# Loading the first group of a rotation in eight transfers of every eighth row

## The chip, the cores and the metric

One core of one Trainium2 chip. The metric is the device time of one execution in microseconds (us), median of several runs. The span in a profile is the time from the first to the last instruction, some 1.8 us shorter than the device time here.

## The reference

```python
x: float32 [32, 3, 256, 256]
return np.rot90(x, k=2, axes=(-2, -1))      # each 256 x 256 image turned by 180 degrees
```

An image of 65,536 elements is simply reversed. 25.17 MB are read and 25.17 MB written, and there is no arithmetic. x and the result lie in HBM, the chip's main memory. The tiles of the kernel lie in SBUF, the core's on-chip memory, and have 128 partitions each. DMA engines move the data between the two; the page counts 16 of them.

## The kernel before

The 96 images are three groups of 32. An image is cut into four rows of 16,384 elements (64 KB), so a group is a tile of 128 partitions, one row each. VectorE reverses each row inside its partition (three copies for each of four pairs of pieces), and the store puts the four rows of an image back in reverse order. Three tiles A, Bt and Ct hold the three groups.

```python
def load(t, g, lo, hi, queue=nc.sync):
    return queue.dma_start(out=t[:, lo:hi], in_=x4[g][:, lo:hi])
...
TAIL = 1536
HEAD = 512
load(A, 0, 0, HEAD, nc.scalar)          # ACT's queue: 512 columns of every row
load(A, 0, HEAD, E)                     # SyncE's queue: the rest
load(Bt, 1, 0, E)
body = load(Ct, 2, 0, E - TAIL)
load(Ct, 2, E - TAIL, E)
inside(A)                               # VectorE, twelve copies
store(A, 0, 0, LEAD)
first = store(A, 0, LEAD, E)            # made to wait for body
...                                     # then inside and store for Bt and Ct
```

## Time and profile before

| | before |
|---|---|
| device time | 122.06 us (121.93 to 122.1, 3 runs) |
| span | 120.2 us |
| busy share of the DMA engines | 97.6% |
| busy share of VectorE | 37% |
| a row of 64 KB on one DMA engine | 2.42 us |

Read it as a stream: six group transfers (three loads, three stores) of about 19.35 us, one behind the other, with about 1.75 us ahead of the first data and 1.4 us behind the last. VectorE's work lies beside it. The profile's lines are shown in the prediction.

### The profile page before, as it was taken

What the parts mean: (1) busy time and instruction counts of PE and PEld (TensorE: products, weight loads), DVE (VectorE), ACT (ScalarE), POOL (GpSimd) and SP (SyncE); (2) the same over time, 40 slices, a digit from 0 to 9 for tenths busy, and PEclk for the clock granted to TensorE, in tenths of its full rate; (3) what the DMA queues carried; (4) which work ended last, traced back from release to release, by engine and by line L of the source; (5) the groups of instructions that cost most, each with busy time, mean ns of one, the idle gap of its engine ahead of it and who ended that gap; (6) DMA issues with size and microseconds to landing.
All of it is one profiled execution on the core that took longest, in us unless ns stands there. A gap on an engine that the chain in (4) does not pass through costs nothing.

```text
span 120.2 us, 97 instructions
## 1 busy us (share of the span) xinstructions
DVE 44.2 (37%) x36; POOL 0.2 (0%) x4
## 2 busy tenths in 40 slices
DVE  0000000499995099999059999500000000000000
POOL 0000000000000000000000000000000000000000
DMA  9888988899889879979499777988898889888990
GB/s 338 349 349 349 698 349 349 360 654 393 349 349 633 382 316 553 395 316 633 178 452 693 346 346 346 693 349 349 349 698 349 349 349 698 349 349 349 654 393 0
DMA packets 1296, 50.33 MB, mean 419 GB/s; under 512 B 144, under 2 KB 272, under 8 KB 528
## 3 DMA queue, kind: packets, MB, share of 16 engines
q1 hardware_dynamic: 1152, 50.07, 97.0%
q10 hardware_dynamic: 144, 0.26, 0.6%
HBM read 25.17 MB, written 25.17 MB: 419 GB/s over the span
## 4 chain that ended last, share of the span: by engine, by line
DMA 34%; DVE 25%; another core or an unknown queue 4%; issue 1%; SPq 0%; DVEq 0%
DMA Bt<-in_x_dram 34%; DVE T L52 8%; DVE Bt L52 8%; DVE Ct L52 8%; SPq L55 0%; DVEq L52 0%
## 5 line engine op out<-in xcount | busy, mean ns | idle before, releaser
L52 DVE COPY T<-A 128x2048 f32<-128x2048 f32 x4 | 4.9, 1226 | 22.7 <-DMA A<-in_x_dram 22.6
L52 DVE COPY T<-Ct 128x2048 f32<-128x2048 f32 x4 | 4.9, 1227 | 4.5 <-DMA Ct<-in_x_dram 4.4
L52 DVE COPY T<-Bt 128x2048 f32<-128x2048 f32 x4 | 4.9, 1226 | 4.4 <-DMA Bt<-in_x_dram 4.3
L52 DVE COPY Bt<-Bt 128x2048 f32<-128x2048 f32 x4 | 4.9, 1227 | 0.1
L52 DVE COPY A<-A 128x2048 f32<-128x2048 f32 x4 | 4.9, 1227 | 0.1
L52 DVE COPY A<-T 128x2048 f32<-128x2048 f32 x4 | 4.9, 1227 | 0.1
L52 DVE COPY Bt<-T 128x2048 f32<-128x2048 f32 x4 | 4.9, 1227 | 0.1
L52 DVE COPY Ct<-T 128x2048 f32<-128x2048 f32 x4 | 4.9, 1227 | 0.1
L52 DVE COPY Ct<-Ct 128x2048 f32<-128x2048 f32 x4 | 4.9, 1227 | 0.1
L100 POOL MEMSET const-bfloat16-1.0<- 128x1 bf16 x1 | 0.1, 101 | 0.0
L100 POOL MEMSET const-uint8-127<- 128x1 uint8 x1 | 0.1, 101 | 0.0
L100 POOL MEMSET const-float32-0.0<- 128x1 f32 x1 | 0.1, 98 | 0.2 <-issue 0.2
L100 POOL MEMSET const-float32-1.0<- 128x1 f32 x1 | 0.1, 98 | 0.0
## 6 DMA issues: line engine op xcount, KB each, us to landing
out_dram<-A SPq DMA_DIRECT2D x1, 8128.0 KB, 21.1
A<-in_x_dram SPq DMA_DIRECT2D x1, 7936.0 KB, 21.9
Ct<-in_x_dram SPq DMA_DIRECT2D x1, 7424.0 KB, 57.9
Ct<-in_x_dram SPq DMA_DIRECT2D x1, 768.0 KB, 59.3
A<-in_x_dram ACTq DMA_DIRECT2D x1, 256.0 KB, 22.0
out_dram<-A SPq DMA_DIRECT2D x1, 64.0 KB, 35.2
Bt<-in_x_dram SPq DMA_DIRECT2D x1, 40.8
out_dram<-Bt SPq DMA_DIRECT2D x1, 39.8
```

The source lines that it names most:

```text
L52: tc.keep_in_program_order(nc.vector.tensor_copy(out=dst, in_=src))
L100: nc = _bacc.Bacc("TRN2", target_bir_lowering=False, num_devices=1)
```

## The change

Its intent, as far as the code tells it: a first transfer of 16 rows has one row for each of the 16 DMA engines, so they might be fed sooner than by a transfer of 128 rows; and ACT's small strip becomes needless. Strip b holds the rows b, b + 8, ..., b + 120, on both sides.

```diff
     def load(t, g, lo, hi, queue=nc.sync):
-        return queue.dma_start(out=t[:, lo:hi], in_=x4[g][:, lo:hi])
+        return tc.keep_in_program_order(
+            queue.dma_start(out=t[:, lo:hi], in_=x4[g][:, lo:hi]))
...
     TAIL = 1536
-    HEAD = 512
-    load(A, 0, 0, HEAD, nc.scalar)
-    load(A, 0, HEAD, E)
+    for b in range(8):
+        tc.keep_in_program_order(
+            nc.sync.dma_start(out=A[b::8, :], in_=x4[0][b::8, :]))
     load(Bt, 1, 0, E)
```

## The prediction

That a row takes 4.84 us, twice 2.42, is an estimate of mine; nothing in the trace of the kernel before shows two engines slowing each other. Nor does it show the 132 us of the second rival.

> **What bounds the kernel now.** I read the page first: span, busy shares, DMA row, queues.
>
> ```profile
> span 120.2 us, 97 instructions
> DVE 44.2 (37%) x36; POOL 0.2 (0%) x4
> ...
> q1 hardware_dynamic: 1152, 50.07, 97.0%
> q10 hardware_dynamic: 144, 0.26, 0.6%
> HBM read 25.17 MB, written 25.17 MB: 419 GB/s over the span
> ```
>
> VectorE works for 44 of 120 us, the DMA engines for 97.0 + 0.6 = 97.6%. q1 is SyncE's queue, q10 ACT's, and q10 carries only the head strip (0.26 MB). The bytes cannot shrink: everything is read once and written once. So the kernel is a stream, and a change shows only where it adds a gap or changes the rate. The windows view, cut at the boundaries of the transfers, shows both (columns: stretch, length, VectorE and POOL busy, clock, DMA share, GB/s; a packet counts where it starts).
>
> ```profile
> 0.00:1.70 1.70, 0.00 (x0) 0.20 (x4) 1.00 0.00 0
> 1.70:21.78 20.08, 0.00 (x0) 0.00 (x0) 1.00 1.00 417
> 21.78:41.15 19.37, 14.72 (x12) 0.00 (x0) 1.00 1.02 440
> ...
> 80.11:99.45 19.34, 0.00 (x0) 0.00 (x0) 1.00 1.00 434
> 99.45:118.80 19.35, 0.00 (x0) 0.00 (x0) 1.00 1.00 434
> 118.80:120.20 1.40, 0.00 (x0) 0.00 (x0) 1.00 0.01 0
> ```
>
> Line two is the first group (8.39 MB), line three the second, the next two are stores. A full-rate group takes 19.35 us, 434 GB/s, which is 27.1 GB/s for each of 16 engines. A group is 128 rows of 64 KB, eight per engine, so a row takes 19.35 / 8 = 2.42 us. The first group takes 0.7 us more (20.08). Finer windows say where:
>
> ```profile
> 0.00:1.75 1.75, 0.00 (x0) 0.20 (x4) 1.00 0.00 0
> 1.75:2.75 1.00, 0.00 (x0) 0.00 (x0) 1.00 2.89 952
> 2.75:3.75 1.00, 0.00 (x0) 0.00 (x0) 1.00 0.15 63
> 3.75:4.75 1.00, 0.00 (x0) 0.00 (x0) 1.00 0.00 0
> 4.75:7.17 2.42, 0.00 (x0) 0.00 (x0) 1.00 1.00 433
> ```
>
> Nothing moves before 1.75; the first row of each engine occupies it to about 4.75, 3.0 us in place of 2.42; then it is steady. So the avoidable time in this kernel is about 1.75 us of start, 0.6 us of first row and 1.4 us of end, 3.7 us together. Last, who waits for the data (the timeline):
>
> ```profile
> 0.73 0.39 SPq L55 DMA_DIRECT2D A<-in_x_dram  x1
> 1.18 0.42 SPq L55 DMA_DIRECT2D Bt<-in_x_dram  x1
> ...
> 22.62 1.23 DVE L52 COPY T<-A 128x2048 f32<-128x2048 f32 x1 [22.62 <-DMA A<-in_x_dram]
> ```
>
> One issue costs SyncE about 0.45 us (0.73 to 1.18). VectorE starts when all of the first group has landed and finishes its twelve copies at about 37.7, well before the store of that group can flow at 60: queue order puts all loads ahead of the stores. VectorE is not on the path.
>
> [...]
>
> **The change, part by part.**
>
> Removed: ACT's strip of 512 columns. Its bytes now ride in the full rows. 0.26 MB at 434 GB/s is 0.6 us, against 0.6% of 120.2 = 0.7 us for q10: a saving of at most 0.1 us.
>
> Moved: the first issue is smaller (16 rows, not 128). If the engines are fed sooner by it, the start shrinks by some tenths; the issue is 0.39 us long, so I take 0.1 to 0.3 us, a guess.
>
> Added: seven more transfers. 8 issues x 0.45 = 3.6 us on SyncE, all during the first rows: an issue comes every 0.45 us, an engine uses one up in 2.42 us. The compiled order also shows new waits: [...] the second group's load now waits for the first strip, the third group's two parts for the second and third strip, the first store for the others. When the first strip lands, seven are still queued, at least 7 x 2.42 = 17 us of work: no gap. VectorE's first copy waits for eight landings in place of two, the last of which is the end of the group as before. Seven more completions per engine: I allow 0.1 us.
>
> Changed without being named: which partitions are written together. Strip b covers partitions b, 8+b, ..., 120+b. For b = 0 these are 0, 8, 16, 24, then 32, 40, 48, 56, then 64 and so on. [...] a row takes 4.84 us, the group 8 x 4.84 = 38.7 us, plus the 0.6 us of the first row, against 20.08 - 0.08 now: +19.3 us.
>
> Nothing hides this. The loads are one queue, so everything behind starts 19.3 us later: first copy near 41.9, second group landed near 60, third near 80, stores from 80 to 138. VectorE again finishes each group before its store's turn, so nothing else is added and nothing is recovered. Sum: 122.06 + 19.3 + 0.1 - 0.2 = 141.3 us.
>
> **The rivals.**
>
> *[...] 121.9 us.* If what limits at 27.1 GB/s is the DMA engine alone [...] the stage takes 19.4 + 0.6, and only the edges move, a few tenths. [...] I give this 0.19.
>
> *A conflict that sorts itself out: about 132 us.* [...] this, or a partial conflict, makes the low end of my range.
>
> *A starved queue.* If the new semaphore waits or eight short transfers left gaps, each strip would add up to the 0.8 us between the end of the first group's packets and the copy (21.78 to 22.62), 6 us in all. Against it: strips are queued before earlier ones land. Chance small.
>
> *Fewer engines than 16 per strip*: time would be in the hundreds; I give it one per cent, within "slower".
>
> *Faster by 2%* needs 2.4 us out of 3.7 us of edges, most of which (first data at 1.75, completion at the end) the change does not touch: 0.01.
>
> **Range and chances.** Slower has all the conflict cases: 0.80. Most of it is the fair case, 139 to 143; the unfair or partial ones spread to 130. [...] I set the top at 144. Range 130 to 144, which leaves out the case of no conflict knowingly.
>
> **What would show it.** Right: the first group's load at about 217 GB/s with DMA share still near 1 (packets twice as long, not gaps), VectorE's first copy near 41.9 us, second group and stores at 434 GB/s and 19.35 us as before; span near 139.5. Wrong: the first copy at about 22.5 (no conflict), or at about 32 (sorted out). [...] If the DMA share falls under 0.9 in the first stage, it is the queue that starves. If the first packets come well before 1.75, the smaller first issue is worth more than I took.

## The result, and the profile after

143.47 us (143.29 to 143.64, 6 runs) against 122.01 us for the kernel before in the same rounds: 21.5 us slower. The ratio is 1.176 (95% interval 1.174 to 1.178). A ratio here is the mean time of one kernel's fast runs over that of the other's of the same rounds, so not quite the ratio of the medians quoted. Predicted were 141.3 us.

The page of the changed kernel, the same lines as before:

```profile
span 141.6 us, 108 instructions
DVE 44.2 (31%) x36; POOL 0.2 (0%) x4
...
q1 hardware_dynamic: 1264, 50.33, 97.6%
HBM read 25.17 MB, written 25.17 MB: 355 GB/s over the span
```

The DMA engines are as busy as before, 97.6% of a span that is 21.4 us longer, for the same bytes. So no gap was added: the packets themselves take longer. The windows view says which (stretch, length, VectorE, POOL, clock, DMA share, GB/s):

```profile
0.00:2.10 2.10, 0.00 (x0) 0.20 (x4) 1.00 0.00 0
...
6.40:11.51 5.11, 0.00 (x0) 0.00 (x0) 1.00 1.00 205
11.51:16.62 5.11, 0.00 (x0) 0.00 (x0) 1.00 1.00 205
16.62:21.73 5.11, 0.00 (x0) 0.00 (x0) 1.00 1.00 205
21.73:26.64 4.91, 0.00 (x0) 0.00 (x0) 1.00 1.01 214
26.64:31.75 5.11, 0.00 (x0) 0.00 (x0) 1.00 1.00 205
...
41.97:61.32 19.35, 14.72 (x12) 0.00 (x0) 1.00 1.03 434
```

Each line of the middle is one strip: the 16 engines take one row each, in 5.11 us in place of 2.42, at 205 GB/s in place of 434. The fifth strip takes 4.91 us; that is a clue for later. The last line is the second group, at full rate again. And the first line shows that no data moves before 2.10 us: the start became later than the 1.75 us of before, not earlier.

The timeline at the start and at VectorE's first copy:

```profile
0.73 5.05 SPq L72 DMA_DIRECT2D A<-in_x_dram  x8
8.71 0.35 SPq L56 DMA_DIRECT2D Bt<-in_x_dram  x1
...
44.25 1.23 DVE L52 COPY T<-A 128x2048 f32<-128x2048 f32 x1 [44.25 <-DMA A<-in_x_dram]
```

The eight issues take 5.05 us, 0.63 us each, more than the 0.45 us of a large transfer. The second group's load is issued at 8.71, when the first strip has landed (8.0 us after its issue at 0.73), and the first copy starts at 44.25 in place of 22.62 us: +21.6 us. All of the loss has happened by then.

### The profile page after: what moved, and what is told of

Its sections match the earlier page's.

```text
span 141.6 us, 108 instructions
## 1 busy us (share of the span) xinstructions
DVE 44.2 (31%) x36; POOL 0.2 (0%) x4
## 3 DMA queue, kind: packets, MB, share of 16 engines
q1 hardware_dynamic: 1264, 50.33, 97.6%
## 4 chain that ended last, share of the span: by engine, by line
DVE 31%; DMA 27%; another core or an unknown queue 6%; SPq 3%; issue 1%; DVEq 0%
DMA A<-in_x_dram 27%; DVE T L52 10%; DVE Ct L52 7%; DVE Bt L52 7%; DVE A L52 7%; SPq L72 3%; DVEq L52 0%
```

## The experiments

My theory: which partitions are written at the same time decides how fast a row goes; in the changed kernel every two engines get about the rate of one (5.11 / 2.42 = 2.1), and with neighbouring partitions every four will. The four is an estimate that no run had shown yet. The rivals: short transfers of 16 rows (or the new semaphore waits) are slow in themselves; or reading HBM rows that lie 512 KB apart is slow. The edits below are against the changed kernel; J is 2,048 columns, an eighth of a row. The kernel before took 121.93 to 122.06 us in all these rounds.

**Neighbouring rows.**

```diff
-            nc.sync.dma_start(out=A[b::8, :], in_=x4[0][b::8, :]))
+            nc.sync.dma_start(out=A[16 * b:16 * b + 16, :], in_=x4[0][16 * b:16 * b + 16, :]))
```

> Eight transfers of 16 neighbouring rows in place of every eighth row; right result. [...] a row takes four times 2.42 us with the loss seen in the changed kernel (5.11 / 4.84 = 1.056), about 10.2 us; the first group takes 8 x 10.2 = 82 us, the whole about 122 + 62 = 184 us. Rival, short transfers are slow in themselves: same count and size as the changed kernel, so 143.5 us. Rival, HBM reads 512 KiB apart collide: the rows are now neighbours in HBM, so about 122 us.

Measured: 176.85 us (4 runs), result correct. Two windows of it, one strip each:

```profile
9.20:18.42 9.22, 0.00 (x0) 0.00 (x0) 1.00 1.00 114
18.42:27.66 9.24, 0.00 (x0) 0.00 (x0) 1.00 1.00 113
```

Both rivals fall: the count and size of the transfers are those of the changed kernel, the HBM rows are neighbours, and a row takes nearly four times as long as at full rate (9.24 / 2.42 = 3.8). The size is off: 9.24 us and not 10.2, and so 176.85 us and not 184.

The two runs that write neighbouring partitions (this one and the second of the pair below) also tell why the start of the changed kernel came late: here the first data moves between 1.70 and 1.80 us, as in the kernel before and in the runs of one transfer and of columns below, and in the changed kernel between 2.05 and 2.15. So stepping over partitions delays the first data, and a first transfer of 16 rows in place of 128 brings it no sooner.

**One transfer of 128 rows by SyncE.**

```diff
-    for b in range(8):
-        tc.keep_in_program_order(
-            nc.sync.dma_start(out=A[b::8, :], in_=x4[0][b::8, :]))
+    load(A, 0, 0, E)
```

> The first group by SyncE in one transfer of 128 full rows, no ACT strip: only the second half of the change. All theories: 122.0 us within 0.3. If it is over 123, losing the ACT strip has a cost of its own and the eight transfers carry less than the 21.4 us.

Measured: 122.14 us (5 runs), ratio 1.0019 (1.0006 to 1.0031). ACT's strip is worth about 0.2 us, and leaving it out is no part of the 21 us worth telling.

**The two sides taken apart**, both wrong (rows permuted). First, neighbouring rows of HBM into every eighth partition:

```diff
-            nc.sync.dma_start(out=A[b::8, :], in_=x4[0][b::8, :]))
+            nc.sync.dma_start(out=A[b::8, :], in_=x4[0][16 * b:16 * b + 16, :]))
```

> Reads 16 neighbouring rows of HBM and writes them to every eighth partition; wrong result on purpose (rows permuted). [...] the partitions are those of the changed kernel, so 143.5 us, a row 5.1 us. Collisions in HBM: about 122 us. Short transfers: 143.5 us.

Measured: 143.34 us (4 runs). Second, every eighth row of HBM into neighbouring partitions:

```diff
-            nc.sync.dma_start(out=A[b::8, :], in_=x4[0][b::8, :]))
+            nc.sync.dma_start(out=A[16 * b:16 * b + 16, :], in_=x4[0][b::8, :]))
```

> Reads every eighth row of HBM and writes 16 neighbouring partitions; wrong result on purpose. [...] as with 16 neighbouring rows on both sides, a row about 10.2 us and about 184 us in all. Collisions in HBM: 143.5 us as the changed kernel. Short transfers: 143.5 us.

Measured: 176.95 us (4 runs). The time follows the partitions alone: which rows of HBM are read changes 143.47 to 143.34 and 176.85 to 176.95 us, within the spread of the runs.

**Eight transfers that reach all partitions.**

```diff
-            nc.sync.dma_start(out=A[b::8, :], in_=x4[0][b::8, :]))
+            nc.sync.dma_start(out=A[:, b * J:(b + 1) * J], in_=x4[0][:, b * J:(b + 1) * J]))
```

> Eight transfers again, same bytes each, but each of all 128 rows and 2048 columns (8 KB of a row). [...] about 122.2 us (64 packets per engine in place of 8, some 8 ns more each, +0.4 us). Short transfers or the new semaphore waits are what costs: about 143 us, or at least clearly over 124.

Measured: 122.29 us (6 runs), ratio 1.0019 (1.0001 to 1.0037). Eight transfers, the same bytes in each, and a wait of the second group's load for the first of them, as in the changed kernel: all that costs about 0.2 us. (The 8 ns a packet of the expectation can be checked in the packet records of the traces: a row in one packet takes 2.418 us, in the two packets of the kernel before 2.342 + 0.084, and in eight packets here 8 x 0.309 = 2.47 us.)

**Four transfers of 32 rows.**

```diff
-    for b in range(8):
+    for b in range(4):
         tc.keep_in_program_order(
-            nc.sync.dma_start(out=A[b::8, :], in_=x4[0][b::8, :]))
+            nc.sync.dma_start(out=A[b::4, :], in_=x4[0][b::4, :]))
```

> Four transfers of 32 rows, every fourth row each: [...] an engine has two rows of each. [...] about 122 us; [...] it is about 143.5 us. Short transfers: between 122 and 143.5, about half the cost. It tells how rows are dealt to engines, not which theory holds.

Measured: 122.61 us (4 runs), ratio 1.0049. Its windows:

```profile
0.00:2.05 2.05, 0.00 (x0) 0.20 (x4) 1.00 0.00 0
...
5.00:7.42 2.42, 0.00 (x0) 0.00 (x0) 1.00 1.01 433
```

Full rate, the 122 us of the two answers: there is no sign that two engines slow each other, although each transfer holds partitions 32 apart, which do so in the next run (7.32 us for two rows, against 5.12 when 64 apart). If each engine were dealt two neighbours of the list and took them in order, the first transfer would begin with the sixteen rows of strip 0 of the changed kernel, at 5.11 us a row; it took 2.42. So the rows are not dealt in that way; in which way was not shown. The start is as late as in the changed kernel (2.05 us), which accounts for some 0.3 of the 0.6 us.

**Single transfers.** One transfer at a time, each waiting for the one before; neighbouring rows of HBM throughout, only the step between partitions differs. Its output is wrong, which doesn't matter for the time. Which steps would be slow was an estimate of mine that no run had shown. The core of it, one source line each:

```python
# rows(t, n, step): n partitions of t, from 0, so many apart
alone(nc.sync.dma_start(out=rows(A, 2, 64), in_=x4[0][0:2, :]))     # L86
... # L87: 2 rows, 32 apart   L88: 2, 4 apart    L89: 2, 1 apart
... # L90: 8, 4 apart   L91: 8, 8 apart   L92: 8, 1 apart
... # L93: 16, 8 apart  L94: 16, 1 apart  L95: 16, 7 apart
alone(nc.sync.dma_start(out=flat[0][0:2, :], in_=rows(A, 2, 64)))   # L96, a store
... # L97: 2, 32 apart  L98: 8, 4 apart   L99: 8, 8 apart   L100: 16, 8 apart
```

> Transfers one at a time, each waiting for the one before; wrong result on purpose. The rows of HBM are neighbours in all of them, only the step between SBUF partitions differs. [...] the time from issue to landing is a fixed part (about 2.5 us) plus a row time: 2 rows 64 or 4 apart 2.4 us, 2 rows 32 or 1 apart 5.1 us; 8 rows 4 apart 2.4, 8 apart 5.1, neighbouring 10.2 us; 16 rows 8 apart 5.1, neighbouring 10.2, 7 apart 5.1 for the slowest pair; then stores, open whether reading SBUF shares in the same way: 2 rows 64 apart 2.4, 32 apart 5.1 if so, 8 rows 4 apart 2.4, 8 apart 5.1 if so, 16 rows 8 apart 5.1 if so. Short transfers are slow in themselves: the row time depends on the number of rows only, not on the step.

Its timeline (start, duration of the issue). From one start to the next is one transfer with its fixed part:

```profile
22.74 0.69 SPq L86 DMA_DIRECT2D A<-in_x_dram  x1
27.86 0.49 SPq L87 DMA_DIRECT2D A<-in_x_dram  x1
35.18 0.59 SPq L88 DMA_DIRECT2D A<-in_x_dram  x1
40.24 0.29 SPq L89 DMA_DIRECT2D A<-in_x_dram  x1
47.24 0.68 SPq L90 DMA_DIRECT2D A<-in_x_dram  x1
52.26 0.58 SPq L91 DMA_DIRECT2D A<-in_x_dram  x1
59.73 0.28 SPq L92 DMA_DIRECT2D A<-in_x_dram  x1
70.90 0.56 SPq L93 DMA_DIRECT2D A<-in_x_dram  x1
78.48 0.33 SPq L94 DMA_DIRECT2D A<-in_x_dram  x1
90.08 0.55 SPq L95 DMA_DIRECT2D A<-in_x_dram  x1
97.29 0.56 SPq L96 DMA_DIRECT2D out_dram<-A  x1
101.31 0.52 SPq L97 DMA_DIRECT2D out_dram<-A  x1
107.92 0.69 SPq L98 DMA_DIRECT2D out_dram<-A  x1
112.16 0.56 SPq L99 DMA_DIRECT2D out_dram<-A  x1
118.87 0.52 SPq L100 DMA_DIRECT2D out_dram<-A  x1
```

Subtract neighbouring starts. Loads of two rows: 5.12 us when 64 apart, 7.32 when 32 apart, 5.06 when 4 apart, 7.00 when neighbours. Two rows on two engines in all four (the trace has two packets at a time), and yet 2 us between them. So it is the partitions that decide: 0 and 32 slow each other, and 0 and 1; 0 and 64, or 0 and 4, do not. Eight rows: 5.02 us when 4 apart, 7.47 when 8 apart (each row then has another one 32 away), 11.17 when neighbours. Sixteen rows: 7.58 us when 8 apart, 11.60 when neighbours. Stores behave in the same way: 4.02 and 6.61 us for two rows 64 and 32 apart, 4.24 and 6.71 us for eight rows 4 and 8 apart, 6.73 us for sixteen rows 8 apart (the next store starts at 125.60). Two sizes were missed. Neighbouring rows, eight or sixteen, were expected at about 12.7 us with the fixed part and took 11.17 and 11.60; and the fixed part itself, expected at 2.5 us, comes out as about 2.6 for loads (5.06 - 2.42) and 1.6 for stores (4.02 - 2.42).

Sixteen rows 7 apart took 7.21 us, near the expected 7.6, but not for the expected reason. The 5.1 us were meant for the slowest pair alone. The windows view gives a DMA share of 0.61 over these 7.21 us, so 4.4 us for the mean row on 16 engines; eight rows 4 apart have 0.29 over 5.02 us, so 2.9 us. In the packet records none of the sixteen is under 3.8 us. So all sixteen rows were slow and not one pair; the reason was not shown.

The issue is longer too when partitions are stepped over: 0.49 to 0.69 us here, against 0.28 to 0.33 us for neighbours; the eight issues of the changed kernel take 5.05 us together, those with neighbouring rows 3.85. It goes with the late start of the changed kernel.

**Other choices of 16 rows.** Is the row time of 5.11 us, in place of twice 2.42 = 4.84, a matter of which rows are written together? Every second row of a block of 32 (no two of them 32 apart), and every fourth row of a half (p and p + 32 again, but in one half of the partitions):

```diff
+        lo = 32 * (b // 2) + b % 2
         tc.keep_in_program_order(
-            nc.sync.dma_start(out=A[b::8, :], in_=x4[0][b::8, :]))
+            nc.sync.dma_start(out=A[lo:lo + 31:2, :], in_=x4[0][lo:lo + 31:2, :]))
```

> Eight transfers of 16 rows, every second row of a block of 32; right result. [...] a row 5.11 us, 143.4 us in all. If the loss of 0.27 us a row over 4.84 belongs to the pair p and p+32 of the changed kernel: 4.84 us a row, about 141.3 us. [...]

Measured: 143.27 us (4 runs), and again 5.11 us a row in its windows.

```diff
+        lo = 64 * (b // 4) + b % 4
         tc.keep_in_program_order(
-            nc.sync.dma_start(out=A[b::8, :], in_=x4[0][b::8, :]))
+            nc.sync.dma_start(out=A[lo:lo + 61:4, :], in_=x4[0][lo:lo + 61:4, :]))
```

> Eight transfers of 16 rows, every fourth row of one half of the partitions; right result. [...] 143.4 us, a row 5.11 us. If the number of halves reached matters besides: other than 143.4 by over 2 us.

Measured: 143.28 us (4 runs). Three quite different choices of rows give the same time within 0.2 us.

**The order of the strips.** The fifth strip of the changed kernel took 4.91 us. Strips 0 to 3 hold the first four partitions of each eight and strips 4 to 7 the last four, so the fifth is the only one that goes over from the one half to the other. If going over is what saves the 0.2 us, doing so in every strip should make all of them 4.91. With neighbouring rows each strip lies 16 partitions away from the one ahead of it, and rows 16 apart did not slow each other (they are among the eight rows 4 apart, 5.02 us). Strips 32 apart, one right after the other, should bring back the missing 1 us, as two rows 32 apart did slow each other (7.32 us). Both are guesses; no run had shown the like.

```diff
-    for b in range(8):
+    for b in (0, 2, 1, 3, 4, 6, 5, 7):
         tc.keep_in_program_order(
-            nc.sync.dma_start(out=A[b::8, :], in_=x4[0][b::8, :]))
+            nc.sync.dma_start(out=A[16 * b:16 * b + 16, :], in_=x4[0][16 * b:16 * b + 16, :]))
```

> The eight transfers of 16 neighbouring rows in the order 0, 2, 1, 3, 4, 6, 5, 7, [...] Then the second transfer of each pair takes about 10.2 us a row, the first about 9.24, and the whole gets 4 x 1 us longer, about 180.8 us. Rival, [...] nothing changes, 176.9 us.

Measured: 178.09 us (4 runs). Its windows, strip by strip:

```profile
9.05:18.70 9.65, 0.00 (x0) 0.00 (x0) 1.00 1.00 109
18.70:28.05 9.35, 0.00 (x0) 0.00 (x0) 1.00 1.00 112
28.05:37.70 9.65, 0.00 (x0) 0.00 (x0) 1.00 1.00 109
```

Right in direction, the strips 32 partitions away from the one ahead being the slower ones (9.65 us, against 9.35), but not in size: about 9.6 us and not 10.2, and 1.2 us in all and not 4. (The profile is of the slowest of the four runs, 178.84 us, so its windows may be a little long.)

```diff
-    for b in range(8):
+    for b in (0, 4, 1, 5, 2, 6, 3, 7):
```

> The changed kernel with the strips in the order 0, 4, 1, 5, 2, 6, 3, 7, [...] about 6 x 0.2 = 1.2 us less, 142.2 us. Rival, the 4.91 us row has another cause: 143.4 us.

Measured: 142.23 us (4 runs), and a strip in its windows:

```profile
11.35:16.25 4.90, 0.00 (x0) 0.00 (x0) 1.00 1.00 214
```

As expected to the tenth. The order of the strips moves the time by 1.2 us, in the expected direction both times. That is shown; the reason is not. If it were that an engine ahead of another has an easier time, the gain should differ with the lead. But the size was missed in the run before, and here the packet records have all rows of the steady strips at 4.88 to 4.95 us, although the engines of one strip start up to 1.2 us apart. So the reason stays open.

No version beat the kernel before; the two nearest are the single transfer and the eight column transfers, both about 0.2% behind.

## Why the prediction was right or wrong

The time was in the range, just above the 139 to 143 us given to the fair case, and the course of the run held step by step. The top of 144 us left room for a row somewhat longer than 4.84 us, and that is what came.

*The bound.* Right: a stream that is never idle, in which only the rate of the first stage changed; the DMA share stayed at 97.6%.

*What is removed and moved.* The strip through ACT was taken as a saving of at most 0.1 us; doing that part alone cost about 0.2 us. The earlier start of 0.1 to 0.3 us, called a guess, was wrong in sign: the first data moved at 2.10 in place of 1.75 us, a delay that only the runs with stepped partitions show. The eight issues took 5.05 us and not 3.6, but behind rows already under way.

*What is added.* Right: the new waits leave no gap. Eight transfers over all partitions, with such waits, cost 0.2 us.

*Two engines at the rate of one.* An estimate when it was made, and about right. It is shown from three sides: the time follows the SBUF side only (143.47 and 143.34 us with every eighth partition, 176.85 and 176.95 with neighbours, whichever rows of HBM are read); a row takes 2.42 us in a transfer of all partitions, 5.11 with every eighth one and 9.24 with 16 neighbours; and in single transfers two rows are enough to see it (5.06 us when 4 apart, 7.00 when neighbours). The 16 rows 7 apart stay unexplained.

*Mis-sized term.* "a row takes 4.84 us", twice the full-rate row, measured 5.11 us in six of the seven steady strips and 4.91 in one. That is 6 x 0.27 + 0.07 = 1.7 of the 2.2 us by which 141.3 fell short of 143.5. The other 0.5 us lies in the later start, the first row and the landing, which I did not separate. Why two engines together get only 205 / 8 = 25.6 GB/s, and not the 27.1 of one at full rate, stays open: it is not a matter of these very rows (two other choices of 16 gave the same time), and with neighbouring rows four engines together get 4 x 65,536 bytes / 9.6 us = 27.3 GB/s where strips lie 32 apart (28.4 at 9.24 us), so it is not a loss that grows as rows get slower.

*Nothing hides it.* Right: the second group ran at 434 GB/s as before, and VectorE again finished each group before its store's turn. The first copy started at 44.25 us, not at 41.9, for the reason above.

*The rivals.* The one without a conflict (121.9 us) and the starved queue fell with the changed kernel's own windows: 5.11 us a row at a DMA share of 1.00. The conflict that sorts itself out did not come, but the order of the strips does count: 0.2 us less for a strip that goes over to the other half of each eight partitions, for a reason that was not shown.

## What to carry to other kernels

When a load or store is cut by partitions, ask which partitions each piece holds, not only how many engines it uses: of the loads here, 16 rows on 16 engines ran at 205 GB/s with partitions 8 apart and at 113 with neighbours, in place of 434, while 32 rows 4 apart ran at 433. Stores cut by partitions were tried as single transfers only: two rows took 4.02 us when 64 partitions apart and 6.61 when 32 apart. Cutting by columns, with all 128 partitions in each of eight pieces, cost next to nothing (0.2%). A DMA share near 100% does not mean full rate (97.6% went with 419 GB/s over the span before and 355 after); read the GB/s beside it.
